# The last product's operand split is moved into the fourth product, the last norm is spread out and done in place, and two tiles are moved by 32 bytes

## The chip, the cores and the metric

One core of one Trainium2 chip runs the kernel. The metric is the device time in microseconds (us) of one execution, given as the median of several runs. The engines are TensorE (PE in the profile, with PEld for its weight loads), VectorE (DVE), ScalarE (ACT), GpSimd (POOL) and SyncE (SP, which here only issues DMAs).

## The reference

A layer on x of 1024 positions by 1024 features: a token mixer (three head groups, one input projection, one output projection), then a feed-forward block. The change touches the second half:

```python
h = rms_norm(x, g_pre_ff[l]) * (1.0 + sc2) + sh2
f = jnp.square(jax.nn.relu(h @ w_ff1[l])) @ w_ff2[l]
x = x + gt2 * rms_norm(f, g_post_ff[l])
```

`w_ff1` is 1024 x 4096, `w_ff2` 4096 x 1024, all in float32. `rms_norm` of `f` needs the sum of squares over all 1024 features of a position before any element can be scaled.

## The kernel before, in words

**Three matmuls for one.** Float32 operands are split into a high and a low part (fp32r): ScalarE casts the high part (`act_hi`), VectorE subtracts it from the raw value to get the low part. `mm3` then issues three matmuls: high by high, high by low, low by high.

**Seven products for eight.** Both feed-forward matmuls cut their operands into 2 x 2 blocks and compute seven products (M1 to M7) on sums of blocks in place of eight. FF1 (16 blocks b of features, 7 x 12 = 84 matmuls of 512 columns each; 14 of the blocks come in the main loop) takes as moving operand either the tile `HL` (the split `h` itself) or `hc` (sums of its blocks), and as weights `wc`. It writes its squared outputs to DRAM as `Y`. FF2 runs the products in the order M1, M5, M6, M4, M7, M3, M2; each adds over 16 values of b, 12 matmuls for each b. A unit `FF2(q, b)` has three steps: `load` (DMAs of a block of Y and of weights into `R`, 1024 columns; where weights are subtracted, a third DMA into `o`), `prep` (subtraction `R<-R,o`, then the split) and `step` (matmuls). The first six products split into pool tiles `x` and use 512 columns.

**The last product, M2**, splits its right operand (block b21 of Y) into `HL`, whose old content is no longer needed, and its weights into tiles `w`, which are kept. It runs in 256-column pieces: piece 0 over all 16 b's, then piece 1 over the same `HL` and `w`, m by m. Its loads and splits stand in the same queues, unit after unit, as all others.

**The last norm** goes in three column pieces, pc 0 (columns 0 to 511, complete when M3 is), pc 1 (512 to 767) and pc 2 (768 to 1023). `square(pc, j)` squares a quarter of the piece into `fq` (ScalarE), adds it to an earlier one, and scales `big` by the gain `g2` in place (ScalarE). `preload(pc)` reads the residual back from `out_dram` into tiles `xh`. `finish` sums over the partitions by matmuls with `ones` (`r<-ones,fq`), takes root and reciprocal, spreads the result by a matmul on a diagonal (`r<-dgt,ones`), multiplies `big` by it into `res`, adds `xh`, and writes `res` out. `FW` is a delay in program order: so much other work is issued before the next part. `behind()` places the norm's matmuls between those of the products.

**Order.** Every engine runs its instructions in the written order. A loop over units calls `load` some units ahead of `step` (`LA`: 5 in FF2) and `prep` 3 ahead. In M2's unit b = 0 the kernel before issues all four `square(0, j)`, `preload(0)` and the start of `finish` for pc 0. Tiles come from a pool: `t` (4 KB, for R, x, w, xh, res), `r` (4 buffers, for o), `h`. `HL` and `big` are fixed tiles ahead of the pool.

Of the kernel before, what the change touches and what calls it, by code (L numbers as in the profile page):

```python
# [21 lines left out]
RS = ((4.1, 2.0, 3.1, 2.1, 4.2), (3.1, 2.0, 2.6, 1.1, 3.7), (2.6, 2.0, 2.6, 0.6, 0.7))  # L22
SEQ = 'f0 f1 z02 a0 a1 b0 b1 z12 z42 z52'
WE = 'GGGGGGGG'
GD = ('GG GG GG GG', 'GV GV', 'V V V V')
NS = (2, 2, 4)
SEs = 'VGV'
FW = (3.5, 4.5, 1.5)
WB = (768,)
LA = (9, 2, 5, 3)  # L30
HY = (2.1, 0.7, 1.4)
REs = ('VG', 'VG', 'VV')
XEs = ('GV', 'VG', 'GV')
# [22 lines left out]
def trunk(ctx, tc, xT, c, pv, ident, w_ada, w_k, w_in, w_v, gates, k1, k2, k3, gmft, w_out, w_ff1, w_ff2, out):  # L56
# [6 lines left out]
    def tt(name, dt=F32, n=1024):  # L63
        return pool.tile([128, n], dt, tag="t", name=name)
# [4 lines left out]
    def pb(name="pb"):  # L69
        return psum.tile([128, 512], F32, tag="b", name=name)  # L70
# [8 lines left out]
    def ctile(name, n, dt=F32, bufs=1):  # L79
        return const.tile([128, n], dt, name=name, tag=name, bufs=bufs)  # L80
# [1019 lines left out]
    class FF2:  # L1100
# [3 lines left out]
        def load(self):  # L1104
            q, b = self.q, self.b
            ra, rb = w_ff2[2 * b], w_ff2[2 * b + 1]
            a11, a12, a21, a22 = ra[:, 0:512], rb[:, 0:512], ra[:, 512:1024], rb[:, 512:1024]
            R = self.R = tt("R")
            self.o = pool.tile([128, 512], F32, tag="r", name="o", bufs=4) if q in ("M5", "M6", "M7", "M3") else None
            nc.sync.dma_start(out=R[:, 0:512], in_=Y[b][:, YB[XS[q]], :])  # L1110
            two = {"M1": (a11,), "M2": (a12,), "M4": (a22,), "M5": (a21, a22), "M6": (SS[b][:, 0, :], a11),
                   "M7": (a11, a21), "M3": (a12, SS[b][:, 1, :])}[q]
            ld[0] = nc.sync.dma_start(out=R[:, 512:1024], in_=two[0]).ins
            if self.o is not None:
                ld[0] = nc.sync.dma_start(out=self.o, in_=two[1]).ins

        def prep(self):
            q, b, R = self.q, self.b, self.R
            w = R[:, 512:1024]
            if self.o is not None:  # L1120
                V.tensor_tensor(out=w, in0=w, in1=self.o, op=ADD if q == "M5" else SUB)  # L1121
                if q in ("M5", "M6"):
                    nc.sync.dma_start(out=SS[b][:, 0 if q == "M5" else 1, :], in_=w)
            if q == "M2":
                x = HL[:, b // 2, b % 2, :]
                act_hi(x[:, 0:512], R[:, 0:512])
                V.tensor_tensor(out=x[:, 512:1024], in0=R[:, 0:512], in1=x[:, 0:512], op=SUB)
                t = hlsplit(w, V, "w2")
                self.X, self.W = (x[:, 0:512], x[:, 512:1024]), t
            else:  # L1130
                hi, lo = wide(R, "x2")
                self.X, self.W = (hi[:, 0:512], lo[:, 0:512]), (hi[:, 512:1024], lo[:, 512:1024])

        def step(self):
            q, b = self.q, self.b
# [38 lines left out]
                mm3([o], wh[:, cs], wl[:, cs], [xs], b == 0 and m % 2 == 0, b == 15, m % 2 == 1)  # L1174


    SE = [{'V': V, 'G': G}[c] for c in SEs]
    sums = {0: [], 1: [], 2: []}

    def square(pc, j):  # L1180

        lo, hi = PIECE[pc]
        g = 512 // (hi - lo)
        a = big[:, j * g:j * g + g, lo:hi]
        q = th("fq")
# [21 lines left out]
    def finish(sums, lo, hi, wait, spec, hold=()):  # L1207
        n = hi - lo
        g, c = 512 // n, n // 128
        spec = spec.split()  # L1210
        xin, at = xins[lo], 8 * lo
        r = pb("r3")
        yield wait
        if lo in WB:
            parts = [t[:, e * n:e * n + n] for t in sums for e in range(g)]
            with behind():
                for j, t in enumerate(parts):
                    mm(r[:, 0:n], ones, t, j == 0, j == len(parts) - 1)
            rr = th("rr", F32, n)
            A.activation(out=rr, in_=r[:, 0:n], func=AF.Sqrt, scale=1.0 / D, bias=eps)  # L1220
            V.reciprocal(rr, rr)
        else:
            with behind():
                for i in range(c):
                    parts = [t[:, e * n + i * 128:e * n + i * 128 + 128] for t in sums for e in range(g)]
                    for j, t in enumerate(parts):
                        mm(r[:, i:i + 1], t, ones[:, 0:1], j == 0, j == len(parts) - 1)
            sd = ctile("sd", 8, bufs=4)
            dg = th("dgt", F32, n)
            A.activation(out=sd[:, 0:c], in_=r[:, 0:c], func=AF.Sqrt, scale=1.0 / D, bias=eps)  # L1230
# [9 lines left out]
        m, rs = 0, None  # L1240
        for i, q in enumerate(spec):
            res = tt("res", F32, 512 * len(q))
            for j, e in enumerate(q):
                o = res[:, j * 512:j * 512 + 512]
                src = rr
                if e in "QR" and lo not in WB:
                    if rs is None:
                        rs = th("rs", F32, n)
                        A.copy(rs, rr)
                    src = rs  # L1250
                (G if e in "QR" else V).tensor_tensor(  # L1251
                    out=o.rearrange("p (m s) -> p m s", m=g), in0=big[:, m:m + g, lo:hi],
                    in1=src.unsqueeze(1).to_broadcast([128, g, n]), op=MUL)
                (G if e in "GQ" else V).tensor_tensor(out=o, in0=o, in1=xin[i][:, j * 512:j * 512 + 512], op=ADD)  # L1254
# [32 lines left out]
    LD1, LP1, LD2, LP2 = LA  # L1287
# [159 lines left out]
```

## Time and profile before

| what | us |
|---|---|
| median of 3 runs (lowest, highest) | 1057.7 (1057.0, 1058.6) |
| the profiled execution | 1055.82 |
| its span | 1054.0 |
| PE busy in it | 981.3 (93%) |
| DVE, ACT, POOL busy in it | 760.6, 507.5, 143.0 |
| 16 DMA engines: mean rate | 182 GB/s |

The span runs from the first to the last instruction that the profiler recorded; 1.8 us of the profiled execution lie around it. Busy times are those of one execution. FF1 and the seven products of FF2 fill the span from 394.81 us to 1039.4 us; the output of the last norm piece ends it.

### The profile page before, as it was taken

How to read it: one execution, taken by the hardware profiler on the slowest of the kernel's cores; microseconds unless marked ns; L12 is line 12 of the kernel's file. 1: busy time of each engine (PE TensorE's matmuls, PEld its weight loads, DVE VectorE, ACT ScalarE, POOL GpSimd, SP SyncE). 2: the span in 40 equal slices, each digit the busy share in tenths (PEclk: the TensorE clock that was granted, in tenths of full speed). 3: DMA queues.
4: the chain of work that ended last, by engine and by line, in shares of the span. 5: the costliest groups of instructions: out<-in, count | busy, mean ns of one | idle time of the engine just before them, and what ended most of it. 6: DMA issues, size and time to landing. Idle time of an engine off the chain costs nothing.

```text
span 1054.0 us, 13168 instructions
## 1 busy us (share of the span) xinstructions
PE 981.3 (93%) x4780; PEld 812.0 (77%) x4780; DVE 760.6 (72%) x1043; ACT 507.5 (48%) x772; POOL 143.0 (14%) x94
## 2 busy tenths in 40 slices
PE   6889976997899999999999999999999999999795
PEld 2668764895678988988888888888888888888685
DVE  7978888778795698896667667676665666577654
ACT  4454777623453455555445445455434444355431
POOL 4400391330320340000000000000000000000231
PEclk8989988998899999999999999999999999999898
DMA  8740210266343432163533433368998877778362
GB/s 344 279 145 11 76 40 0 72 247 233 108 157 123 141 110 86 47 229 131 198 114 143 183 130 144 146 240 295 357 396 305 309 255 260 249 225 312 130 210 91
DMA packets 80003, 191.59 MB, mean 182 GB/s; under 512 B 8769, under 2 KB 13121, under 8 KB 77890
## 3 DMA queue, kind: packets, MB, share of 16 engines
q1 hardware_dynamic: 76482, 186.56, 50.1%
q10 hardware_dynamic: 3456, 4.20, 1.1%
q8 instruction: 37, 0.61, 0.2%
q14 instruction: 28, 0.23, 0.1%
HBM read 144.58 MB, written 46.14 MB: 181 GB/s over the span
## 4 chain that ended last, share of the span: by engine, by line
PE 73%; DVE 13%; DMA 5%; ACT 4%; issue 2%; POOL 1%; SPq 0%; DVEq 0%; POOLq 0%; ACTq 0%
PE f L142 56%; PE op L142 7%; PE zk L142 4%; DVE raw L453 3%; DMA raw<-in_w_ada_dram 3%; PE z L142 2%; PE r L142 2%; DMA R<-in_w_ff_dram 1%; PE grs L142 1%; DVE xr L480 1%; DVE big L536 1%; ACT av L518 1%; DMA xh<-in_xT_dram 1%; DVE ti L538 1%; DMA big<-in_xT_dram 1%
## 5 line engine op out<-in xcount | busy, mean ns | idle before, releaser
L142 PE MATMUL f<-x,x 128*128 128x512 f32 x768 | 236.4, 389 | 0.0
L142 PEld LDWEIGHTS f<-x,x 128*128 128x128 f32 x768 | 144.2, 188 | 29.9
L936 ACT CAST x<-R 128x1024 fp32r<-128x1024 f32 x96 | 100.7, 1054 | 128.3 <-DVE R L1121 62.9
L142 PE MATMUL f<-HL,wc 128*128 128x512 f32 x672 | 161.8, 396 | 0.0
L142 PE MATMUL f<-x 128*128 128x512 f32 x384 | 149.5, 389 | 0.0
L142 PEld LDWEIGHTS f<-HL,wc 128*128 128x128 f32 x672 | 125.1, 188 | 31.5 <-ACT big L1066 2.2
L947 DVE TENSOR_TENSOR x<-R,x 128x1024 fp32r<-128x1024 f32 x96 | 116.6, 1220 | 25.6 <-ACT x L936 22.4
L142 PE MATMUL f<-hc,wc 128*128 128x512 f32 x504 | 119.6, 391 | 0.0
L142 PEld LDWEIGHTS f<-hc,wc 128*128 128x128 f32 x504 | 94.7, 188 | 20.7
L1254 POOL TENSOR_TENSOR res<-res,xh 128x512 f32<-128x512 f32 x10 | 16.3, 1653 | 601.9 <-DVE res L1251 601.9
L142 PE MATMUL op<-HL,hi 128*128 128x256 f32 (+1 forms) x384 | 88.0, 323 | 0.0
L1121 DVE TENSOR_TENSOR R<-R,o 128x512 f32<-128x512 f32 x64 | 44.3, 692 | 59.9 <-DMA R<-in_w_ff_dram 36.9
L142 PEld LDWEIGHTS f<-x 128*128 128x128 f32 x384 | 72.1, 188 | 14.9
L142 PEld LDWEIGHTS op<-HL,hi 128*128 128x128 f32 x384 | 63.5, 188 | 7.3 <-issue 1.4
L170 POOL TENSOR_TENSOR lo<-raw,hi 128x1024 fp32r<-128x1024 f32 x16 | 44.1, 2766 | 158.1 <-ACT hi L169 111.8
L142 PE MATMUL z<-HL,hi 128*128 128x512 f32 x192 | 64.9, 441 | 0.7 <-ACT ftg L613 0.7
L142 PE MATMUL op<-HL,lo 128*128 128x256 f32 (+1 forms) x192 | 61.4, 320 | 0.0
L453 DVE SCALAR_TENSOR_TENSOR raw<-raw,cond 128x1024 f32<-128x1024 f32 x32 | 49.9, 1567 | 13.4 <-DMA raw<-in_w_ada_dram 13.4
L936 ACT CAST wc<-S 128x1024 fp32r<-128x1024 f32 x28 | 29.4, 1052 | 60.7 <-DVE S L1041 57.2
L142 PE MATMUL f<-HL,w 128*128 128x256 f32 x384 | 49.5, 288 | 2.5 <-DVE w L941 2.3
L142 PEld LDWEIGHTS f<-HL,w 128*128 128x128 f32 x384 | 47.5, 194 | 3.9 <-DVE w L941 2.9
L947 DVE TENSOR_TENSOR wc<-S,wc 128x1024 fp32r<-128x1024 f32 x28 | 34.2, 1221 | 21.8 <-PE f L142 20.0
(299 smaller groups left out, 1695.3 us busy)
## 6 DMA issues: line engine op xcount, KB each, us to landing
R<-Y SPq DMA_DIRECT2D x112, 256.0 KB, 4.6
raw<-in_w_ada_dram SPq DMA_DIRECT2D x48, 512.0 KB, 4.7
R<-in_w_ff_dram SPq DMA_DIRECT2D x96, 256.0 KB, 4.5
raw<-in_w_ff_dram SPq DMA_DIRECT2D x32, 512.0 KB, 3.2
Y<-big SPq DMA_DIRECT2D x16, 1024.0 KB, 3.9
o<-in_w_ff_dram SPq DMA_DIRECT2D x48, 256.0 KB, 5.0
Y<-big SPq DMA_DIRECT2D x13, 768.0 KB, 3.5
SS<-R SPq DMA_DIRECT2D x32, 256.0 KB, 5.0
```

What stands on the lines that cost most here:

```text
L142: pe[0] = T.matmul(o, w, x, start=start, stop=stop, skip_group_check=more).ins
L170: (eng or V).tensor_tensor(out=lo, in0=src, in1=hi, op=SUB)
L453: V.scalar_tensor_tensor(out=r, in0=r, scalar=0.5, in1=cond, op0=MUL, op1=MUL, accum_out=mod[:, blk:blk + 1])
L480: V.scalar_tensor_tensor(out=xr[:, o0:o1], in0=z[:, i0:i1], scalar=col("conv_w", k * 4 + t), in1=xr[:, o0:o1], op0=MUL, op1=ADD)
L518: A.activation(out=av[:, a:b], in_=rr[h], func=AF.Exp, scale=m4[:, i:i + 1], bias=m4[:, i:i + 1])
L536: V.tensor_tensor_scan(ti, av, ti, 0.0, op0=MUL, op1=ADD)
L538: V.tensor_tensor_scan(ti[:, ::-1], av[:, ::-1], ti[:, ::-1], 0.0, op0=MUL, op1=ADD)
L936: order[0] = A.copy(dst, src).ins
L947: V.tensor_tensor(out=lo, in0=raw, in1=hi, op=SUB)
L1121: V.tensor_tensor(out=w, in0=w, in1=self.o, op=ADD if q == "M5" else SUB)
L1254: (G if e in "GQ" else V).tensor_tensor(out=o, in0=o, in1=xin[i][:, j * 512:j * 512 + 512], op=ADD)
```

## The change

It does five things.
- M4 (the fourth product) loads block b21 of Y beside its own operands, into `o`, and splits it into `HL` there (16 casts, 16 subtractions). M2 then loads only weights (256 KB per unit, into `o`, for 512 KB into `R`) and splits only these. `LA` gets two more numbers: loads 7 units ahead and preps 4 ahead for M2's 16 units.
- The squares of pc 0 are spread over M2's units b = 1 to 4; `preload(0)` and `finish` for pc 0 start at b = 7. All additions of squares are on VectorE, into one tile for a piece (two for pc 2), so that there are fewer norm matmuls.
- The gain g2 of pc 0 is no longer multiplied on ScalarE but inside `finish`, in one VectorE instruction with the norm's factor.
- `finish` works in place: `big` times the factor into `big`, plus `xh` into `xh`, which is written out. `res` is gone, and so is all work of GpSimd at the end.
- 32 bytes are put ahead of `HL` and 32 behind `big`. As built, `HL` moves from address 3456 to 3488, `big` from 68992 to 69024, and the pool's first tile from 102240 to 102304 (in each partition).

```diff
@@ constants and tiles @@
-GD = ('GG GG GG GG', 'GV GV', 'V V V V')
-NS = (2, 2, 4)
-SEs = 'VGV'
+GD = ('VV VV VV VV', 'VV VV', 'V V V V')
-LA = (9, 2, 5, 3)
+LA = (9, 2, 5, 3, 7, 4)
+    ctile("pad0", 8)
     HL = const.tile([128, 8, 2, 1024], F32R, name="HL", tag="HL")
     big = const.tile([128, 8, 1024], F32, name="big", tag="big")
+    ctile("pad1", 8)
@@ FF2.load @@
...
+            self.o = pool.tile([128, 512], F32, tag="r", name="o", bufs=4) if q != "M1" else None
+            if q == "M2":
+                ld[0] = nc.sync.dma_start(out=self.o, in_=a12).ins
+                return
...
-            two = {"M1": (a11,), "M2": (a12,), "M4": (a22,), "M5": (a21, a22), "M6": (SS[b][:, 0, :], a11),
+            two = {"M1": (a11,), "M4": (a22, Y[b][:, YB["b21"], :]), "M5": (a21, a22),
...
@@ FF2.prep @@
+            x = HL[:, b // 2, b % 2, :]
+            if q == "M2":
+                self.X, self.W = (x[:, 0:512], x[:, 512:1024]), hlsplit(self.o, V, "w2")
+                return
...
-            if q == "M2":
-                x = HL[:, b // 2, b % 2, :]
-                act_hi(x[:, 0:512], R[:, 0:512])
-                V.tensor_tensor(out=x[:, 512:1024], in0=R[:, 0:512], in1=x[:, 0:512], op=SUB)
-                t = hlsplit(w, V, "w2")
-                self.X, self.W = (x[:, 0:512], x[:, 512:1024]), t
...
+            if q == "M4":
+                act_hi(x[:, 0:512], self.o)
+                V.tensor_tensor(out=x[:, 512:1024], in0=self.o, in1=x[:, 0:512], op=SUB)
@@ square @@
-        if len(sums[pc]) < NS[pc]:
+        if not sums[pc] or (pc == 2 and j == 1):
             sums[pc].append(q)
         else:
-            i = j % NS[pc]
-            SE[pc].tensor_tensor(out=sums[pc][i], in0=sums[pc][i], in1=q, op=ADD)
-        for m in range(j * g, j * g + g):
+            V.tensor_tensor(out=sums[pc][0], in0=sums[pc][0], in1=q, op=ADD)
+        for m in range(j * g, j * g + g if pc else 0):
             A.activation(out=big[:, m, lo:hi], in_=big[:, m, lo:hi], func=AF.Copy, scale=g2[:, m:m + 1])
@@ finish @@
...
-            res = tt("res", F32, 512 * len(q))
...
+                o, x = big[:, m:m + g, lo:hi], xin[i][:, j * 512:j * 512 + 512]
+                if g == 1:
+                    V.scalar_tensor_tensor(out=o[:, 0], in0=o[:, 0], scalar=g2[:, m:m + 1], in1=rr, op0=MUL, op1=MUL)
+                else:
+                    V.tensor_tensor(out=o, in0=o, in1=rr.unsqueeze(1).to_broadcast([128, g, n]), op=MUL)
+                (G if e == "G" else V).tensor_tensor(out=x.rearrange("p (m s) -> p m s", m=g), in0=o,
+                                                     in1=x.rearrange("p (m s) -> p m s", m=g), op=ADD)
...
-            nc.sync.dma_start(out=out[:, at:at + 512 * len(q)], in_=res)
+            nc.sync.dma_start(out=out[:, at:at + 512 * len(q)], in_=xin[i])
@@ the loop over units @@
...
+    def ahead(u, a, b, c):
+        return a if u < n1 else b if u < len(units) - 16 else c
...
-        while lo_ <= u + LD2 and (lo_ <= u + LD1 or lo_ >= n1):
+        while lo_ <= u + ahead(lo_, LD1, LD2, LD3):
...
-            for j in range(4):
-                square(0, j)
-            preload(0)
-            tf = [spawn(finish(sums[0], 0, 512, FW[0], GD[0]), 0.0)]
+        if o.q == "M2":
+            if 1 <= o.b < 5:
+                square(0, o.b - 1)
+            if o.b == 7:
+                preload(0)
+                tf = [spawn(finish(sums[0], 0, 512, FW[0], GD[0]), 0.0)]
```

On TensorE, in M2's piece 0, the sums of pc 0's squares stood behind the third unit (each unit has twelve matmuls, two rows; `w_...` names its weights):

```order
L142 MATMUL f_7666<-HL,w_7638 128x256 x6
L142 MATMUL r_7696<-ones,fq 128x1 x8
L142 MATMUL f_7665<-HL,w_7662 128x256 x6
L142 MATMUL f_7666<-HL,w_7662 128x256 x6
L142 MATMUL f_7665<-HL,w_7711 128x256 x3
L142 MATMUL r_7696<-dgt,ones 128x512
```

Now, at the same place of the program, they stand behind the tenth unit (`w_7648` is the first unit's, `w_7821` the tenth's):

```order
L143 MATMUL f_7724<-HL,w_7821 128x256 x6
L143 MATMUL r_7869<-ones,fq 128x1 x4
L143 MATMUL f_7723<-HL,w_7838 128x256 x6
L143 MATMUL f_7724<-HL,w_7838 128x256 x6
L143 MATMUL f_7723<-HL,w_7855 128x256 x3
L143 MATMUL r_7869<-dgt,ones 128x512
```

The norm's matmuls are seven units later, and four in place of eight.

On VectorE, at the end of M3 (`big<-big,f` adds M3's sums to `big`), half of M2's splits stood ahead of M3's sums, and each needed a block of Y and one of weights; behind the norm the other half followed, between the products of `finish`:

```order
L941 TENSOR_TENSOR w_7784<-R,w_7784 128x512
L1127 TENSOR_TENSOR HL<-R,HL 128x512
L1164 TENSOR_TENSOR big<-big,f_7290 128x512
L1164 TENSOR_TENSOR big<-big,f_7291 128x512
L1164 TENSOR_TENSOR big<-big,f_7292 128x512
L1191 TENSOR_TENSOR fq<-fq 128x512
L1164 TENSOR_TENSOR big<-big,f_7293 128x512
L1191 TENSOR_TENSOR fq<-fq 128x512 x3
L1231 RECIPROCAL sd<-sd 128x4
L1232 TENSOR_TENSOR dgt<-idt,sd 128x512
L1251 TENSOR_TENSOR res<-big,r_7696 128x512 x2
L941 TENSOR_TENSOR w_7810<-R,w_7810 128x512
```

Now the first fourteen splits of weights stand ahead of M3's sums, and the last two between the additions of squares:

```order
L942 TENSOR_TENSOR w_7896<-o,w_7896 128x512
L1170 TENSOR_TENSOR big<-big,f_7355 128x512
L1170 TENSOR_TENSOR big<-big,f_7356 128x512
L1170 TENSOR_TENSOR big<-big,f_7357 128x512
L1170 TENSOR_TENSOR big<-big,f_7358 128x512
L1195 TENSOR_TENSOR fq<-fq 128x512
L942 TENSOR_TENSOR w_7920<-o,w_7920 128x512
L1195 TENSOR_TENSOR fq<-fq 128x512
L942 TENSOR_TENSOR w_7935<-o,w_7935 128x512
L1195 TENSOR_TENSOR fq<-fq 128x512 x2
L1235 RECIPROCAL sd<-sd 128x4
```

No split of M2 is left behind the norm, and none needs Y.

On SP's queue, the four reads of the residual (`xh<-out_dram`, 512 KB each) stood behind the sixth of M2's sixteen pairs of loads:

```order
L1110 DMA R<-Y_3018 128x512
L1113 DMA R<-in_w_ff_dram 128x512
L1203 DMA xh<-out_dram 128x1024 x4
L1110 DMA R<-Y_3019 128x512
L1113 DMA R<-in_w_ff_dram 128x512
```

Now they stand behind the fifteenth of M2's sixteen single loads:

```order
L1120 DMA o<-SS_3046 128x512
L1112 DMA o<-in_w_ff_dram 128x512 x15
L1207 DMA xh<-out_dram 128x1024 x4
L1112 DMA o<-in_w_ff_dram 128x512
```

One load is left behind them, where ten pairs were.

## Rows read from the trace of the kernel before

**Rows 1.** Busy time by stretch of the span. Columns: stretch; its length, then the busy time (and instructions) of PE, PEld, DVE, ACT and POOL; the granted TensorE clock; the share of the DMA engines; GB/s. The stretches are: early products, output projection, FF1, the first six products of FF2, M2.

```profile
100.00:290.00 190.00, 161.92 (x813) 133.57 (x813) 155.21 (x183) 109.77 (x164) 67.66 (x39) 0.90 0.31 109
290.00:412.00 122.00, 117.79 (x708) 102.04 (x708) 93.03 (x167) 57.77 (x124) 31.62 (x27) 1.00 0.40 132
412.00:712.00 300.00, 300.00 (x1394) 246.61 (x1393) 218.81 (x309) 149.84 (x221) 0.00 (x0) 1.00 0.40 151
712.00:974.00 262.00, 262.00 (x1158) 217.07 (x1157) 168.78 (x186) 120.81 (x142) 0.00 (x0) 1.00 0.86 296
974.00:1039.40 65.40, 55.21 (x421) 53.06 (x420) 35.65 (x49) 21.97 (x39) 18.85 (x12) 0.92 0.44 155
```

**Rows 2.** The chain of work that ended last. Columns: start, duration, engine, what.

```profile
412.03 559.26 PE f L142 x2535
971.34 7.13 DMA R<-in_w_ff_dram
...
1039.57 3.47 PE r L142 x16
```

**Rows 3.** Timeline of PE in M2 and the tail. Columns: start, duration, engine, line, operation, output and operands, shape, count; in brackets the idle time before and what ended it. Each float32 norm matmul has two records.

```profile
973.85 4.36 PE L142 MATMUL f<-HL,w 128*128 128x256 f32 x36
985.10 0.59 PE L142 MATMUL r<-ones,fq 128*128 128x1 f32 x2 [6.89 <-DVE fq L1191]
986.38 3.15 PE L142 MATMUL r<-ones,fq 128*128 128x1 f32 x14 [0.69 <-DVE fq L1191]
...
992.73 1.09 PE L142 MATMUL r<-dgt,ones 128*128 128x512 f32 x2
993.26 8.93 PE L142 MATMUL f<-HL,w 128*128 128x256 f32 x71
...
1021.10 1.50 PE L142 MATMUL r<-ones,fq 128*128 128x1 f32 x12
1022.46 1.30 PE L142 MATMUL f<-HL,w 128*128 128x256 f32 x9
1023.70 0.67 PE L142 MATMUL r<-dgt,ones 128*128 128x256 f32 x2
1024.02 15.55 PE L142 MATMUL f<-HL,w 128*128 128x256 f32 x129
1039.40 3.62 PE L142 MATMUL r<-fq,ones 128*128 128x256 f32 x16
```

**Rows 4.** Timeline of SP's queue around the residual reads.

```profile
965.30 4.57 SPq L1203 DMA_DIRECT2D xh<-out_dram  x4
```

**Rows 5.** Timeline of ACT at M2's start.

```profile
976.45 0.62 ACT L936 CAST HL<-R 128x512 fp32r<-128x512 f32 x1 [5.42 <-DMA R<-Y]
```

**Rows 6.** Timeline of DVE at M2's start.

```profile
977.11 0.69 DVE L1127 TENSOR_TENSOR HL<-R,HL 128x512 fp32r<-128x512 f32 x1 [5.35 <-ACT HL L936]
...
980.43 1.88 DVE L1164 TENSOR_TENSOR big<-big,f 128x512 f32<-128x512 f32 x3
```

**Rows 7.** DMA issues of the page: line engine op xcount, KB each, median us from issue to landing.

```profile
o<-in_w_ff_dram SPq DMA_DIRECT2D x48, 256.0 KB, 5.0
...
xh<-out_dram SPq DMA_DIRECT2D x6, 512.0 KB, 6.6
```

**Rows 8.** Timeline of PE where FF1 ends and FF2 begins (columns as in Rows 3): the moving operand changes from `HL` to `x`.

```profile
707.09 5.77 PE L142 MATMUL f<-HL,wc 128*128 128x512 f32 x24
712.69 0.40 PE L142 MATMUL f<-x 128*128 128x512 f32 x1
...
714.09 0.39 PE L142 MATMUL f<-x 128*128 128x512 f32 x1
...
730.41 0.39 PE L142 MATMUL f<-x 128*128 128x512 f32 x1
```

**Rows 9.** Timeline of SP's queue in FF1: the raw weights of two blocks after each other, each load held back until the block before frees its buffers.

```profile
513.08 6.34 SPq L163 DMA_DIRECT2D raw<-in_w_ff_dram  x2
...
532.52 6.34 SPq L163 DMA_DIRECT2D raw<-in_w_ff_dram  x2
```

**Rows 10.** The costliest groups of PE, shapes kept apart: line engine op, names, shapes, count | busy us, mean ns | idle before.

```profile
L142 PE MATMUL f<-HL,wc 128*128 128x512 f32 x672 | 161.8, 396 | 0.0
L142 PE MATMUL z<-HL,hi 128*128 128x512 f32 x192 | 64.9, 441 | 0.7 <-ACT ftg L613 0.7
...
L142 PE MATMUL op<-HL,hi 128*128 128x512 f32 x128 | 41.0, 400 | 0.0
```

**Rows 11.** Timeline of all engines in the tail (columns as in Rows 3).

```profile
1040.39 0.63 ACT L1186 ACTIVATE fq<-big 128x512 f32<-128x512 f32 x1 [9.80 <-DVE big L1343]
...
1043.12 0.47 ACT L1220 ACTIVATE rr<-r,eps 128x256 f32<-128x256 f32 x1 [1.16 <-PE r L142]
```

**Rows 12.** Busy time by stretch as in Rows 1: M4 alone.

```profile
843.00:887.00 44.00, 44.00 (x195) 36.46 (x195) 27.68 (x28) 18.70 (x19) 0.00 (x0) 1.00 0.78 254
```

**Rows 13.** Timeline of DVE in M3: the split of its unit b = 8, and the last two splits.

```profile
946.02 1.23 DVE L947 TENSOR_TENSOR x<-R,x 128x1024 fp32r<-128x1024 f32 x1 [0.94 <-ACT x L936]
...
958.98 2.54 DVE L947 TENSOR_TENSOR x<-R,x 128x1024 fp32r<-128x1024 f32 x2 [0.20 <-ACT x L936]
```

**Rows 14.** Timeline of PE in M3: the first matmuls of its units b = 8 and b = 15.

```profile
952.09 0.39 PE L142 MATMUL f<-x 128*128 128x512 f32 x1
...
971.13 0.39 PE L142 MATMUL f<-x 128*128 128x512 f32 x1
```

More of the change, by code (lines that the diff above doesn't have):

```diff
@@ L1107, in load @@
             a11, a12, a21, a22 = ra[:, 0:512], rb[:, 0:512], ra[:, 512:1024], rb[:, 512:1024]
+            self.o = pool.tile([128, 512], F32, tag="r", name="o", bufs=4) if q != "M1" else None
+            if q == "M2":
+                ld[0] = nc.sync.dma_start(out=self.o, in_=a12).ins
+                return
             R = self.R = tt("R")
-            self.o = pool.tile([128, 512], F32, tag="r", name="o", bufs=4) if q in ("M5", "M6", "M7", "M3") else None
             nc.sync.dma_start(out=R[:, 0:512], in_=Y[b][:, YB[XS[q]], :])
-            two = {"M1": (a11,), "M2": (a12,), "M4": (a22,), "M5": (a21, a22), "M6": (SS[b][:, 0, :], a11),
-                   "M7": (a11, a21), "M3": (a12, SS[b][:, 1, :])}[q]
+            two = {"M1": (a11,), "M4": (a22, Y[b][:, YB["b21"], :]), "M5": (a21, a22),
+                   "M6": (SS[b][:, 0, :], a11), "M7": (a11, a21), "M3": (a12, SS[b][:, 1, :])}[q]
             ld[0] = nc.sync.dma_start(out=R[:, 512:1024], in_=two[0]).ins
@@ L1117, in prep @@
         def prep(self):
-            q, b, R = self.q, self.b, self.R
+            q, b = self.q, self.b
+            x = HL[:, b // 2, b % 2, :]
+            if q == "M2":
+                self.X, self.W = (x[:, 0:512], x[:, 512:1024]), hlsplit(self.o, V, "w2")
+                return
+            R = self.R
             w = R[:, 512:1024]
-            if self.o is not None:
+            if q not in ("M1", "M4"):
                 V.tensor_tensor(out=w, in0=w, in1=self.o, op=ADD if q == "M5" else SUB)
@@ L1123, in prep @@
                     nc.sync.dma_start(out=SS[b][:, 0 if q == "M5" else 1, :], in_=w)
-            if q == "M2":
-                x = HL[:, b // 2, b % 2, :]
-                act_hi(x[:, 0:512], R[:, 0:512])
-                V.tensor_tensor(out=x[:, 512:1024], in0=R[:, 0:512], in1=x[:, 0:512], op=SUB)
-                t = hlsplit(w, V, "w2")
-                self.X, self.W = (x[:, 0:512], x[:, 512:1024]), t
-            else:
-                hi, lo = wide(R, "x2")
-                self.X, self.W = (hi[:, 0:512], lo[:, 0:512]), (hi[:, 512:1024], lo[:, 512:1024])
+            hi, lo = wide(R, "x2")
+            self.X, self.W = (hi[:, 0:512], lo[:, 0:512]), (hi[:, 512:1024], lo[:, 512:1024])
+            if q == "M4":
+                act_hi(x[:, 0:512], self.o)
+                V.tensor_tensor(out=x[:, 512:1024], in0=self.o, in1=x[:, 0:512], op=SUB)
         def step(self):
@@ L1174, in piece @@
                 mm3([o], wh[:, cs], wl[:, cs], [xs], b == 0 and m % 2 == 0, b == 15, m % 2 == 1)
-    SE = [{'V': V, 'G': G}[c] for c in SEs]
     sums = {0: [], 1: [], 2: []}
@@ L1239, in finish @@
         yield from hold
-        m, rs = 0, None
+        m = 0
         for i, q in enumerate(spec):
-            res = tt("res", F32, 512 * len(q))
             for j, e in enumerate(q):
[L1244 to L1254, printed above, removed]
+                o, x = big[:, m:m + g, lo:hi], xin[i][:, j * 512:j * 512 + 512]
[5 more added lines that the diff above has]
+                                                     in1=x.rearrange("p (m s) -> p m s", m=g), op=ADD)
                 m += g
                 yield 0.9
-            nc.sync.dma_start(out=out[:, at:at + 512 * len(q)], in_=res)
+            nc.sync.dma_start(out=out[:, at:at + 512 * len(q)], in_=xin[i])
             at += 512 * len(q)
@@ L1285, in trunk @@
         pend.append(y_out(b, c11, c12, c21, c22, slab(2 + b), [(c12, 0, 1), (c22, 1, 1), (c21, 2, 1)]))
-    LD1, LP1, LD2, LP2 = LA
+    LD1, LP1, LD2, LP2, LD3, LP3 = LA
     units = [(o, i) for o in b1s for i in range(7)][2:] + [(o, None) for o in b2s]
@@ L1302, in do_prep @@
             o.prep() if i is None else o.prep(i)
+    def ahead(u, a, b, c):
+        return a if u < n1 else b if u < len(units) - 16 else c
     lo_, pr_ = 1, 1
     for u, (o, i) in enumerate(units):
-        while lo_ <= u + LD2 and (lo_ <= u + LD1 or lo_ >= n1):
+        while lo_ <= u + ahead(lo_, LD1, LD2, LD3):
             do_load(lo_)
             lo_ += 1
-        while pr_ <= u + LP2 and (pr_ <= u + LP1 or pr_ >= n1):
+        while pr_ <= u + ahead(pr_, LP1, LP2, LP3):
             do_prep(pr_)
```

## The prediction

> **What bounds the kernel now.** I read the busy time by stretch first [rows 1]. From 412 to 974 us PE is busy all the time at a granted clock of 1.00: FF1 and the first six products of FF2 are bound by the issue of matmuls, and only shorter matmuls can shorten them. M2 is different: of 65.40 us PE is busy 55.21, its clock is 0.92, and DVE, ACT and POOL are all far from full. The chain of waits says the same: 559.26 us of matmuls without a break, then a DMA of weights of 7.13 us for M2, and at the end the norm's 16 matmul records [rows 2].
>
> The timeline of PE says where M2 loses [rows 3]. It begins at 973.85 and ends at 1039.40, 65.55 us. Its own products run at (1039.40 - 1024.02) / 129 = 119.2 ns where nothing disturbs them, so 384 of them need 45.8 us. PE stops for 6.89 us ahead of `r<-ones,fq`, which stands behind three units, and waits there for squares. Going back from there: on SP's queue 2 MB of residual reads stand in the middle of M2's loads [rows 4]; ACT idles 5.42 us for a block of Y, and casts it only at 976.45 [rows 5]; DVE, in order, does that unit's splits and the two behind it, and so adds M3's sums to `big` only from 980.43 [rows 6], though M3 ended at about 974. Squares, additions and the norm's matmuls follow. So the stop is a queueing effect and not a lack of data for the products. Behind it PE runs slowly for a while (the norm's 14 records take 3.00 us, 214 ns each; twelve such records take 1.36, 113 each, at 1021.10).
>
> **M2 after.** The products need 45.8 us as before. The norm matmuls inside M2: two groups of 8 records at 113 ns, 1.8 us, and two spreads, 993.26 - 992.73 = 0.53 and 1024.02 - 1023.70 = 0.32, together 2.7 us [rows 3].
>
> Does PE still wait at the first norm? It now comes behind ten units, at 973.85 + 10 x 12 x 0.1192 = 988.2. On DVE fourteen splits of weights stand ahead of M3's sums. There are four `o` buffers; one round of four takes 5.0 us from issue to landing [rows 7] plus a cast of 0.62 and a subtraction of 0.69 (the same shapes as in [rows 5, 6]), 6.3 us. The first four are loaded while M3's last units are split. M3's last split ended at 958.98 + 2.54 = 961.5, 9.6 us before PE needed it [rows 13, 14]. From there four splits take 2.8 us and three more rounds 18.9 at most: the fourteenth is done at about 982, M3's four sums (1.88 us for three) at 984.5. The last two squares stand on ACT behind the cast of the sixteenth load, which waits in the queue for the residual reads: issued at about 977, landed 6.6 us later [rows 7], so about 985, then a load, a cast, two squares and two additions, some 3 us: 988. That is level with PE. I take 0; if M3's splits had only the lead of their worst unit, 952.09 - (946.02 + 1.23) = 4.8 us [rows 13, 14], all of it would come 4 us later, and that is the bound. The products need the last split by 973.85 + 15 x 1.43 = 995, which either case meets.
>
> The second norm: the spread of pc 0 ends at about 991.7, then DVE does 16 in-place instructions at 0.63 us (the sums' time [rows 6]), 10.1 us, before piece 0's sums, squares and additions, some 3.3 us: 1005.1. PE arrives there after 192 products, the first norm and 62 more products: 973.85 + 22.9 + 1.4 + 7.4 = 1005.5. That is level, and I add 0.5 us. The cover is piece 1's products; without it, a DVE late by x makes PE late by x. M2 thus takes 45.8 + 2.7 + 0.5 = 49.0 and **16.5 us** are saved (13 if the first norm waits, 17 with no wait).
>
> **The tail.** Sixteen records of 3.47 / 16 = 217 ns become eight [rows 2]. Four can run before the last square, which ends at 1040.39 + 0.63 = 1041.02; the other four then take 0.9, and the root, now at 1043.12 [rows 11], starts at about 1042.0: **1.1 us**. What follows keeps its eight operations.
>
> **M4's extra work.** M4 gets 16 x 0.62 = 9.9 us on ACT and 16 x 0.69 = 11.0 on DVE. In its 44 us these are busy 18.70 and 27.68 [rows 12], so both fit (28.6 and 38.7). DMA goes from 512 to 768 KB per unit, which the other products carry. PE is covered by the lead of the splits; I cost it at **0**. If the fuller queues cost 0.3 us of lead per unit, 16 units would take 4.8 us, just what M3 has left at its lowest, unit 8 [rows 13, 14]: the bound is a stall of 5 us. In the program as built, `R` of M7 reuses buffers freed five units before and no longer three, which speaks for more lead, not less. FF1's earlier loads change nothing: each already waits for a buffer [rows 9].
>
> **The 32 bytes.** The matmuls with `HL` as moving operand take (712.69 - 707.09) / 24 = 233.3 ns, those with `x`, straight behind them at the same clock, (730.41 - 714.09) / 72 = 226.7 [rows 8]. Both load their weights from the pool; the moving tile differs. Before, `HL` lies 32 bytes off the pool's grid (3456 and 102240, modulo 512), `x` and its weights on one grid; after, `HL` is on it too (3488 and 102304). So I take it that `HL` then gets the time of `x`. An FF1 block has a period of 532.52 - 513.08 = 19.44 us [rows 9]; 84 matmuls at 226.7 would be 19.04: 14 blocks, 5.6 us. The other 512-column matmuls with `HL` at full clock on a busy PE are those of the output projection and the first two FF1 blocks between 290 and 412 us [rows 1, 10], about 260 at 7 ns: 1.8. Those of the early products (`z` and the like, about 400 [rows 10]) lie where the clock is 0.90 and PE idles [rows 1]: 0, bound 2.7. The 256-column ones need 119.2 ns against 113 for the one-column matmuls, so at most 6 ns each can go; for M2's 384 and as many earlier I take 2 ns, 1.5 us, bounds 0 and 5. Sum **8.9 us**, bounds 0 and 15.
>
> [...]
>
> **Sum.** 16.5 + 1.1 + 8.9 = 26.5 us from the profiled execution's 1055.8 (span 1054.0 and 1.8 around it): 1029.3. The median of the runs is 1.9 above that execution, so the median forecast is 1031.
>
> **The rivals.** *The 32 bytes do nothing* (0.20). The 6.6 ns could belong to where `HL` lies or to how its rows are cut, and not to the grid; nothing in this trace varies the address alone. Then 1031 + 8.9 = 1040.
>
> *Part of M2's gain comes back* (0.12). M3's splits lose their lead to M4's loads (5 us), or the fourteen splits ahead of M3's sums come late (4 us): 1035 to 1040. For it speaks the 4.8 us of lead; against it that ten units now lie between.
>
> *Slower* (0.04). The pool moves too, by 64 bytes, so all other matmuls get new addresses. If the 1656 matmuls on `x` and `hc` went up by twice what separates `HL` from `x`, 13.2 ns, and `HL` gained nothing, that is +21.9 on 1040: 1062. It decides from 17.6 / 1656 = 10.6 ns on. Against it: two streams on the pool's grid keep their distance to each other, and they are the fast ones.
>
> *No change* (0.02): M2's stop only moves to the second norm, the clock falls there instead, and the 32 bytes are worth nothing.
>
> **How the numbers follow.** The forecast itself has 0.62, with its own range 1026 to 1035. The range for 8 in 10 goes down to 1024 (the bounds of the 32 bytes) and up to 1042, which takes in the rivals at 1035 to 1040. A measurement of this kernel tells about 0.2% (2 us) from no change: faster 0.62 + 0.20 + 0.12 = 0.94, same 0.02, slower 0.04.
>
> **What the profile after would show.** M2 from its first product to the last norm in about 49 us, no stop of PE over 1 us, clock near 1.00 in it; if a stop ahead of `r<-ones,fq` stays, M3's sums on DVE are late. `HL` streams at 227 ns and an FF1 block in 19.0 us; if 233 and 19.44 stay, the first rival holds. The splits of M3 at least 4 us ahead of PE; if not, M4's extra loads are the cause. POOL idle after 412 us. The prediction is wrong above all if the 32 bytes do something other than bring `HL` to the time of `x`.

## The result and the profile after

The changed kernel takes 1030.3 us (median of 6 runs, 1028.9 to 1033.0) against 1057.35 for the kernel before in the same sittings; the ratio is 0.9752, 95% interval 0.9729 to 0.9775. The forecast was 1031, with a range of 1024 to 1042. The profiled execution took 1031.33, its span is 1029.5. One execution of the kernel a_pool below took 1608.63 us at a mean granted clock of 0.561 and is left out of its figures.

The span by stage, worked out from the start of the first matmul of each stage (the end of M2 is the start of the last norm's first matmul):

| stage | before | after | saved | forecast |
|---|---|---|---|---|
| to FF1's main loop | 440.57 | 438.29 | 2.3 | 1.8 |
| FF1's 14 blocks | 272.12 | 267.61 | 4.5 | 5.6 |
| FF2, six products | 261.16 | 261.12 | 0.0 | 0 |
| M2 | 65.55 | 49.40 | 16.15 | 16.5, and a part of 1.5 for shorter 256-column matmuls in all stages |
| tail | 14.6 | 13.1 | 1.5 | 1.1 |

The longest piece of the changed kernel's chain of waits (start, duration, engine, what) answers to [rows 2], where M2 began with a DMA of 7.13 us. It reaches into M2, and no DMA stands in the chain behind it:

```profile
409.26 572.32 PE f L143 x2667
```

Busy time by stretch (columns as in [rows 1]): M2 in three thirds. PE is busy throughout, and its granted clock is 1.00 where it was 0.92.

```profile
968.00:984.00 16.00, 16.00 (x137) 16.00 (x136) 4.90 (x9) 1.94 (x4) 0.00 (x0) 1.00 0.14 47
984.00:1000.00 16.00, 16.00 (x132) 15.52 (x130) 12.75 (x20) 2.97 (x6) 0.00 (x0) 1.00 0.55 198
1000.00:1016.00 16.00, 15.95 (x131) 15.72 (x131) 6.77 (x12) 1.80 (x4) 0.00 (x0) 1.00 0.29 100
```

The timeline of PE in M2 and the tail, which answers to [rows 3]. There is no bracket (no idle time) before the norm's matmuls; the eight records of each norm's sums take 0.81 us (982.23 - 981.42).

```profile
967.02 14.55 PE L143 MATMUL f<-HL,w 128*128 128x256 f32 x120
981.42 0.95 PE L143 MATMUL r<-ones,fq 128*128 128x1 f32 x8
982.23 2.04 PE L143 MATMUL f<-HL,w 128*128 128x256 f32 x15
984.10 1.02 PE L143 MATMUL r<-dgt,ones 128*128 128x512 f32 x2
984.56 14.84 PE L143 MATMUL f<-HL,w 128*128 128x256 f32 x119
999.23 0.95 PE L143 MATMUL r<-ones,fq 128*128 128x1 f32 x8
...
1001.61 14.97 PE L143 MATMUL f<-HL,w 128*128 128x256 f32 x122
1016.42 1.02 PE L143 MATMUL r<-fq,ones 128*128 128x256 f32 x4
1018.02 1.13 PE L143 MATMUL r<-fq,ones 128*128 128x256 f32 x4 [0.58 <-ACT fq L1191]
```

On DVE (same columns) M3's sums come at 965.77, while M3 still runs, and the last addition of squares ends at 971.84 + 1.48 = 973.3: 8 us before PE asks for it at 981.42. Before, M3's sums came only at 980.43, 6.6 us after M3's end [rows 6].

```profile
965.16 0.69 DVE L942 TENSOR_TENSOR w<-o,w 128x512 fp32r<-128x512 f32 x1 [2.03 <-ACT w L937]
965.77 2.47 DVE L1170 TENSOR_TENSOR big<-big,f 128x512 f32<-128x512 f32 x4
...
971.84 1.48 DVE L1195 TENSOR_TENSOR fq<-fq 128x512 f32<-128x512 f32 x2
```

The change of the moving operand from `HL` to `x`, which answers to [rows 8]: (705.90 - 700.47) / 24 = 226.3 ns for `HL`, where it was 233.3.

```profile
700.47 5.60 PE L143 MATMUL f<-HL,wc 128*128 128x512 f32 x24
705.90 0.39 PE L143 MATMUL f<-x 128*128 128x512 f32 x1
```

SP's queue in FF1, which answers to [rows 9]: a block takes 528.78 - 509.67 = 19.11 us, where it took 19.44.

```profile
509.67 6.25 SPq L164 DMA_DIRECT2D raw<-in_w_ff_dram  x2
...
528.78 6.25 SPq L164 DMA_DIRECT2D raw<-in_w_ff_dram  x2
```

### The profile page after: what moved, and what is told of

It reads as the page before. It is cut to its first block, busy times and chain, and to the rows that moved or that the text cites. A ratio compares the mean times of both kernels' runs of the same rounds, so it can differ in the third digit from the quotient of the medians.

```text
span 1029.5 us, 13104 instructions
## 1 busy us (share of the span) xinstructions
PE 963.3 (94%) x4756; PEld 804.0 (78%) x4756; DVE 766.4 (74%) x1059; ACT 501.0 (49%) x764; POOL 123.8 (12%) x82
## 3 DMA queue, kind: packets, MB, share of 16 engines
q10 hardware_dynamic: 3456, 4.20, 1.1%
## 4 chain that ended last, share of the span: by engine, by line
PE 73%; DVE 14%; DMA 4%; ACT 4%; issue 3%; POOL 1%; SPq 0%; DVEq 0%; POOLq 0%
PE f L143 59%; PE op L143 6%; DMA raw<-in_w_ada_dram 3%; DVE raw L454 2%; PE z L143 2%; PE zk L143 2%; PE grs L143 1%; PE r L143 1%; DVE raw L291 1%; DVE HL L325 1%; DVE xr L481 1%; DVE big L537 1%; DMA big<-in_xT_dram 1%; ACT av L519 1%; DVE ss L279 1%
## 5 line engine op out<-in xcount | busy, mean ns | idle before, releaser
L143 PE MATMUL f<-HL,wc 128*128 128x512 f32 x672 | 158.1, 390 | 0.0
L143 PEld LDWEIGHTS z<-HL,hi 128*128 128x128 f32 x192 | 38.5, 204 | 11.9 <-issue 3.7
```

The source lines that it names most:

```text
L143: pe[0] = T.matmul(o, w, x, start=start, stop=stop, skip_group_check=more).ins
```

## The experiments

### The 32 bytes: distance or place

Four kernels made from the kernel before, with paddings alone (`ctile` counts in floats of 4 bytes, so 8 are 32 bytes):

```diff
+    ctile("pad0", 8)    # p_both, p_ahead
     HL = const.tile([128, 8, 2, 1024], F32R, name="HL", tag="HL")
     big = const.tile([128, 8, 1024], F32, name="big", tag="big")
+    ctile("pad1", 8)    # p_both, p_behind; 24 in p_64
```

> The kernel before with the two paddings of 32 bytes and nothing else. Theory (the distance between HL and the pool, 0 modulo 512 bytes, sets the matmul's time): HL streams of 512 columns at 227 ns where they were at 234, an FF1 block in 19.1 to 19.2 us, FF1 4 us shorter and the output projection and early products 2 to 3 us shorter together; time 1050 to 1052. Rival (the paddings are worth nothing and the shorter streams of the changed kernel come from its other edits): 234 ns stays, 1057.

> The kernel before with the padding behind big alone: HL stays at 3456, the pool moves from 102240 to 102272, so their distance is 0 modulo 512. Theory (the distance counts): 227 ns for HL streams. Rival (HL's own address counts, whether it is a multiple of 64): 234 ns stays.

> The kernel before with the padding ahead of HL alone: HL moves to 3488 and the pool to 102272, so their distance is what it was, 32 short of a multiple of 512. Theory (the distance counts): 234 ns stays, 1057. Rival (HL's own address counts): 227 ns.

> The kernel before with 96 bytes behind big: HL at 3456, the pool at 102336, distance 64 modulo 512. If only the distance modulo 64 counts: 227 ns, as with distance 0. [...]

With both paddings: 1052.75 us, ratio 0.994 (0.9915 to 0.9964). The other three ran once each: p_behind 1052.31, p_ahead 1057.53, p_64 1062.09 us. The groups of PE with shapes kept apart (busy us, mean ns) for p_both, p_behind, p_ahead and p_64 in turn; [rows 10] has 396 for the kernel before:

```profile
L144 PE MATMUL f<-HL,wc 128*128 128x512 f32 x672 | 157.9, 390 | 0.0
```

```profile
L143 PE MATMUL f<-HL,wc 128*128 128x512 f32 x672 | 158.0, 390 | 0.0
```

```profile
L143 PE MATMUL f<-HL,wc 128*128 128x512 f32 x672 | 161.8, 396 | 0.0
```

```profile
L143 PE MATMUL f<-HL,wc 128*128 128x512 f32 x672 | 161.7, 395 | 0.0
```

A mean of 390 goes with a spacing (start to start, median) of 227 ns, 396 with 234, 395 with 233. p_behind leaves `HL` where it was and gains; p_ahead moves `HL` as the change does and does not. So what counts is the distance between the moving operand and the weights: 0 modulo 512 bytes is good, 32 short and 64 over are not. FF1 took 272.12 us before and 267.45 with both paddings: 4.7 us; with p_behind 267.48, with p_ahead 272.21.

A fifth kernel, made from the changed one, tries a distance of 256:

```diff
-    sp = ctile("sp", 64)
...
     ctile("pad1", 8)
+    sp = ctile("sp", 64)
```

> The changed kernel with the tile sp (256 bytes) behind big in place of ahead of HL: HL at 3232, the pool at 102304, distance 256 modulo 512. If the distance counts modulo 256 or less: 227 ns for HL streams of 512 columns, 120 for 256, time 1030. [...]

```profile
L143 PE MATMUL f<-HL,wc 128*128 128x512 f32 x672 | 158.0, 390 | 0.0
```

The time was 1030.26 us (one run), and the spacing is 227 ns again: distance 256 is as good as 0, and by p_64 distance 64 is not. Whether the time repeats in steps of 256 bytes or of 128 was not tried.

### The paddings and the 256-column matmuls

> The changed kernel without the two paddings. Theory (the distance of HL and the pool is worth what it was in the kernel before): HL streams of 512 columns at 234 ns, time 1036 to 1038, M2 unchanged or 0.5 us shorter, since its 256-column matmuls were 118 ns off the grid and 120 on it. Rival (M2's gain needs the paddings): M2 longer than 51 us.

```diff
-    ctile("pad0", 8)
-    ctile("pad1", 8)
```

1036.45 us, ratio 0.9783 (0.9761 to 0.9806). PE's timeline in M2 of this kernel:

```profile
974.16 14.16 PE L141 MATMUL f<-HL,w 128*128 128x256 f32 x120
...
1008.09 14.59 PE L141 MATMUL f<-HL,w 128*128 128x256 f32 x122
1022.52 1.02 PE L141 MATMUL r<-fq,ones 128*128 128x256 f32 x4
```

The last 122 products take (1022.52 - 1008.09) / 122 = 118.3 ns each; in the changed kernel it is (1016.42 - 1001.61) / 122 = 121.4. M2 is 48.36 us here and 49.40 there. The paddings help the 512-column matmuls on `HL` in FF1 (mean 390 ns there, 395 here) and harm the 256-column ones. A further kernel takes both advantages: it keeps FF1 at distance 0 and writes M2's operand 32 bytes further on.

```diff
-    HL = const.tile([128, 8, 2, 1024], F32R, name="HL", tag="HL")
+    HLf = const.tile([128, 16392], F32R, name="HL", tag="HL")
+    HL = HLf[:, 0:16384].rearrange("p (a b c) -> p a b c", a=8, b=2)
...
-            x = HL[:, b // 2, b % 2, :]
+            x = HLf[:, 8 + b * 1024:8 + b * 1024 + 1024]
```

(The padding behind `big` is taken out, so that the pool stays where it is.)

> The changed kernel with HL eight floats longer and M2's right operand written 32 bytes further on in it, so that the 512-column matmuls of FF1 keep the distance 0 and the 256-column ones of M2 get a distance of 32 bytes. Theory (distance 0 is the best one for 512 columns and the worst for 256): HL streams of FF1 stay at 227 ns, M2's matmuls go from 120 to 118 ns, M2 from 49.4 to 48.4 us, time 1 us below the changed kernel, which is less than the runs can tell. Rival (the 118 ns came from the place of the weights in the pool, not from the distance): M2 stays at 49.4.

```profile
965.12 14.16 PE L143 MATMUL f<-HL,w 128*128 128x256 f32 x120
...
999.04 14.59 PE L143 MATMUL f<-HL,w 128*128 128x256 f32 x122
1013.47 1.02 PE L143 MATMUL r<-fq,ones 128*128 128x256 f32 x4
```

M2 takes 1013.47 - 965.12 = 48.35 us, with 118.3 ns for a product, and FF1 stays at 267.6. The rival falls: the weights have not moved. The time was 1028.92 us, ratio 0.972 (0.9683 to 0.9757), which cannot be told from the changed kernel's; the microsecond is seen in the trace alone.

### What frees M2

Three kernels made from the changed one undo the place of the norm, the place of the split, and both. a_norm0:

```diff
-            if 1 <= o.b < 5:
-                square(0, o.b - 1)
-            if o.b == 7:
-                preload(0)
-                tf = [spawn(finish(sums[0], 0, 512, FW[0], GD[0]), 0.0)]
+        if o.q == "M2" and o.b == 0:
+            for j in range(4):
+                square(0, j)
+            preload(0)
+            tf = [spawn(finish(sums[0], 0, 512, FW[0], GD[0]), 0.0)]
```

a_split2 (a_both has this and the edit above):

```diff
-            if q == "M2":
-                ld[0] = nc.sync.dma_start(out=self.o, in_=a12).ins
-                return
-            two = {"M1": (a11,), "M4": (a22, Y[b][:, YB["b21"], :]), "M5": (a21, a22),
+            two = {"M1": (a11,), "M2": (a12,), "M4": (a22,), "M5": (a21, a22),
...
+            if q == "M2":
+                act_hi(x[:, 0:512], R[:, 0:512])
+                V.tensor_tensor(out=x[:, 512:1024], in0=R[:, 0:512], in1=x[:, 0:512], op=SUB)
+                self.X, self.W = (x[:, 0:512], x[:, 512:1024]), hlsplit(w, V, "w2")
+                return
```

> The changed kernel with pc 0's four squares, the residual reads and the start of its norm back at M2's unit b = 0; the right operand stays split in M4. The first norm then stands behind four units in place of ten, at M2's start + 5.8 us; in the changed kernel its data were ready at M2's start + 6.3. Theory (the moved split is what frees VectorE; the norm's later place is only reserve): PE waits 0 to 2 us, time 1030 to 1033. Rival (the later place is what hides the norm): PE waits 5 us or more and its clock falls, 1037 to 1041.

> The changed kernel with the right operand loaded and split in M2 as before (two loads and four splitting operations for a unit), the norm still behind ten units and the residual reads still late. Theory (the split is what delays M3's sums): the sums come 5 to 8 us later than in the changed kernel, the first norm's data at M2's start + 12 to 16, PE waits 0 to 3 us there or for splits, 1031 to 1035. Rival (the place of the norm and of the residual reads alone is enough): no wait, 1030.

> Both of these undone together: split in M2, norm and residual reads at b = 0. Theory (each of the two alone covers the stop, so that their gains do not add): PE stops 6 to 9 us ahead of the first norm, its clock falls, M2 takes 60 to 65 us, 1041 to 1046. Rival (one of them carries the gain alone): the same time as the worse of the two single ones.

| kernel | median us | ratio to the kernel before (95%) | M2 in the profile |
|---|---|---|---|
| after | 1030.3 | 0.9752 (0.9729 to 0.9775) | 49.40 |
| a_norm0 | 1034.62 | 0.9771 (0.9749 to 0.9792) | 53.55 |
| a_split2 | 1036.83 | 0.9792 (0.975 to 0.9835) | 54.43 |
| a_both | 1042.94 | 0.9853 (0.9818 to 0.9888) | 57.74 |
| p_both | 1052.75 | 0.994 (0.9915 to 0.9964) | 67.70 |

The M2 of this table is that of one profiled execution each. The time of a_norm0 lies between its theory (1030 to 1033) and its rival (1037 to 1041), that of a_split2 above both of its own (1031 to 1035, 1030); a_both's is in the range of its theory (1041 to 1046), but its M2 is shorter than 60 to 65 us.

In a_norm0 PE waits 2.60 us for the squares, and then its granted clock is 0.72 for 6 us (PE's timeline; the clock is the number before the DMA share in the second fence):

```profile
975.27 1.05 PE L143 MATMUL r<-ones,fq 128*128 128x1 f32 x8 [2.60 <-DVE fq L1195]
976.19 2.60 PE L143 MATMUL f<-HL,w 128*128 128x256 f32 x11
```

```profile
976.00:982.00 6.00, 6.00 (x33) 5.24 (x34) 2.66 (x5) 0.26 (x1) 0.00 (x0) 0.72 0.01 3
```

The last addition ends 7.9 us after M2's start (975.22 - 967.36) and PE asks 5.3 us after it. In the changed kernel the data are there after 6.3 us, so about 1.0 us of the 2.60 comes from the norm's place alone. The other 1.6 us go with late weights: the residual reads are back in the middle of M2's loads, and a load issued right behind them at 953.46 is cast only at 962.85, 9.4 us later, where such loads took 5.0 from issue to landing in the kernel before [rows 7]. ACT's timeline:

```profile
962.85 2.59 ACT L937 CAST w<-o 128x512 fp32r<-128x512 f32 x4 [5.55 <-DMA o<-in_w_ff_dram]
```

In a_split2 the first norm's sums are in time, but the next step, `dgt`, is not, and PE waits for that. On ACT the last unit's casts stand ahead of the root in the program, and they need a block of Y. That block is loaded behind the residual reads: issued at 975.08, cast at 984.30, 9.2 us later. On DVE that unit's two subtractions stand ahead of `dgt` (PE's timeline, then ACT's and DVE's):

```profile
987.30 2.04 PE L143 MATMUL r<-dgt,ones 128*128 128x512 f32 x2 [3.40 <-DVE dgt L1231]
```

```profile
984.30 0.62 ACT L937 CAST HL<-R 128x512 fp32r<-128x512 f32 x1 [1.48 <-DMA R<-Y]
```

```profile
984.95 0.69 DVE L1125 TENSOR_TENSOR HL<-R,HL 128x512 fp32r<-128x512 f32 x1 [1.40 <-ACT HL L937]
...
986.46 0.69 DVE L1231 TENSOR_TENSOR dgt<-idt,sd 128x512 f32<-128x512 f32 x1
```

With both undone PE stops 5.76 us and its granted clock is 0.54 in the stretch behind (PE's timeline, then the stretch):

```profile
977.78 1.87 PE L143 MATMUL r<-ones,fq 128*128 128x1 f32 x8 [5.76 <-DVE fq L1190]
```

```profile
978.00:984.00 6.00, 6.00 (x27) 5.60 (x27) 2.89 (x6) 1.29 (x3) 0.00 (x0) 0.54 0.36 113
```

In a_both M3's sums on DVE are in time, 0.3 us after M2's start (966.71). What is late are the squares: on ACT they stand behind a cast that waits for a block of Y, again one that was loaded behind the residual reads (issued at 963.95; DVE's timeline, then ACT's):

```profile
967.03 2.48 DVE L1165 TENSOR_TENSOR big<-big,f 128x512 f32<-128x512 f32 x4
```

```profile
971.50 0.62 ACT L937 CAST HL<-R 128x512 fp32r<-128x512 f32 x1 [5.11 <-DMA R<-Y]
```

My expectation of a cover that either edit gives alone fell: in M2 one undone costs 4.2 us, the other 5.0, both 8.3. Whether the gains add is less sure. The profiled execution of a_both was the fastest of its four (1039.37 for a median of 1042.94), and by the ratios to the kernel before (their differences times 1058) the costs are 2, 4 and 11 us, each known to a few us only. Nor are the causes two separate queues: in all three kernels the wait goes back to loads that stand behind the residual reads on SP's queue, and with the split in M2 blocks of Y are among them.

### GpSimd's additions, and what is left

a_both with two more edits undone (b_pool_la), and the changed kernel with GpSimd's additions alone (a_pool):

```diff
-GD = ('VV VV VV VV', 'VV VV', 'V V V V')    # both kernels
+GD = ('GG GG GG GG', 'GV GV', 'V V V V')
-LA = (9, 2, 5, 3, 7, 4)                     # b_pool_la
+LA = (9, 2, 5, 3, 5, 3)
```

> The changed kernel with the residual's additions of pc 0 (all eight) and pc 1 (half) back on GpSimd, still in place. Theory (these additions hurt only where VectorE has splits with two SBUF operands beside them, and here the splits are over by then): M2 stays within 1 us of 49.4, time 1030 to 1031. Rival (GpSimd's additions slow VectorE's in-place products too, and so delay the second norm): second norm's matmuls wait 2 us or more, 1032 to 1035.

> The kernel with both of M2's moves undone (split in M2, norm at b = 0), which ran at a ratio of 0.985 to the kernel before, with two more edits undone: the additions of pc 0 and half of pc 1 on GpSimd again, and loads and preps of M2 5 and 3 units ahead again. What is left of the change against the kernel before is the paddings, the sums on VectorE into one tile, the gain in the norm's instruction and the missing res tiles. Theory (GpSimd's additions stretch the splits beside them, and shorter look-ahead starves them): M2 64 to 68 us, 1049 to 1053. Rival (the res tiles and ScalarE's scaling were what cost): M2 58 to 61 us, 1040 to 1044.

a_pool: 1030.19 us, ratio 0.9731 (0.9677 to 0.9784), which cannot be told from the changed kernel's; M2 1015.94 - 966.83 = 49.11 us. PE's timeline:

```profile
966.83 8.44 PE L143 MATMUL f<-HL,w 128*128 128x256 f32 x69
...
1015.94 1.02 PE L143 MATMUL r<-fq,ones 128*128 128x256 f32 x4
```

Taking GpSimd out of the end is worth nothing that these runs can tell once no split stands beside it. b_pool_la: 1045.29 us, ratio 0.9873 (0.9833 to 0.9914), M2 63.38 us. It lies between my two expectations, and its interval overlaps that of a_both. GpSimd's additions do stretch the splits beside them, to as much as 1.79 us here and 1.78 in the kernel before (DVE's timeline; the same subtraction takes 0.69 alone, and the products of `big` and `r` between them take 0.67 to 0.69 in the kernel before), but PE waits only 0.46 us for one of them; the larger part is the first stop (PE's timeline, then DVE's):

```profile
993.54 1.79 DVE L1125 TENSOR_TENSOR HL<-R,HL 128x512 fp32r<-128x512 f32 x1
995.25 1.79 DVE L942 TENSOR_TENSOR w<-R,w 128x512 fp32r<-128x512 f32 x1
```

```profile
980.73 1.87 PE L143 MATMUL r<-ones,fq 128*128 128x1 f32 x8 [10.74 <-DVE fq L1190]
```

```profile
970.06 0.69 DVE L1125 TENSOR_TENSOR HL<-R,HL 128x512 fp32r<-128x512 f32 x1 [5.00 <-ACT HL L937]
```

GpSimd has no part in that stop: it ends at 980.73, and GpSimd's first addition in M2 starts at 988.00. On DVE splits that wait for late blocks of Y stand ahead of M3's sums here, which come 9.2 us after M2's start (973.39 - 964.20); in a_both they came after 0.3. That points to the look-ahead, which was not changed alone. The stop also differs from kernel to kernel with the same M2: in one execution each of the kernel before and of p_both, p_behind, p_ahead and p_64 it was 6.89, 8.51, 11.18, 9.43 and 10.69 us, and M2 65.6 to 71.5. So of the 5.6 us between b_pool_la and a_both (63.38 and 57.74) 5.0 are the first stop (10.74 and 5.76), by the look-ahead or by this spread, and 0.46 the wait beside GpSimd's additions.

Between p_both and b_pool_la (1052.75 and 1045.29) lie the sums of squares on VectorE into fewer tiles, with fewer norm matmuls, the gain in the norm's instruction and the missing `res` tiles. Of it the traces show the tail (1.5 us) and the norm matmuls of M2, which after the stop take 1.7 us for 8 records and 0.8 for the next 8, where p_both's 16 and 16 took 4.3 and 1.8. That is 3.6 of the 4.3 us between their M2s (67.70 and 63.38). The edits were not tried one by one.

## Why the prediction was right, and where its steps were off

**The place and the sum.** M2's loss was read right: it was PE's idle time and what went with it. M2 fell to 49.40 us; forecast were 49.0, or about 48.2 with its half of the 1.5 us for shorter 256-column matmuls. Of the 16.15 us saved, 10.2 were idle time of PE (65.40 - 55.21 in [rows 1], nothing over 0.1 us now), 3.8 the sums of the norm (5.4 us for 32 records, 1.6 for 16), and 2.1 the products, which took 49.1 us with a part at the lower clock and take 46.9. FF1 moved by the length of its matmuls and the six products of FF2 not at all. Total forecast 26.5 us, measured between the two profiled spans 24.5, between the medians 27.

**The first norm** was put level with PE (988 us on the old scale, bound 4 us late). It came 8 us early. The step that failed is the place of M3's last split: I kept it where it was, 12.3 us ahead of M2's start (961.5 and 973.85), and let the fourteen splits take up to 21.7 us from there. It ended 19.5 us ahead (947.52 and 967.02), and the fourteen took 18.3, so that they are over at 965.85, before M3 ends:

```profile
946.30 1.22 DVE L948 TENSOR_TENSOR x<-R,x 128x1024 fp32r<-128x1024 f32 x1 [1.16 <-ACT x L937]
947.44 2.49 DVE L942 TENSOR_TENSOR w<-o,w 128x512 fp32r<-128x512 f32 x4
```

The moved split itself gives M3 this lead: in the changed kernel M3's splits end 12.7 us or more before PE's first matmul of the unit (in a_norm0 12.4, in a_pool 12.2, in a_nopad 11.5), where the least was 4.8 in the kernel before; with the split back in M2 it is 2.3 in a_split2, 4.8 in a_both and 3.3 in b_pool_la. The prediction only remarked that M7's buffers speak for more lead, and gave it no time.

**The second norm** was put level too, with 0.5 us: there is no idle time before its sums at 999.23, but its last addition ends only at 998.84, so this term was read rightly and there is 0.4 us to spare. **M4's extra work** was put at nothing, and the six products take 261.12 us for 261.16. It did cost lead: M4's splits end at least 6.1 us ahead of PE, where it was 11.6.

**The tail.** 1.1 us forecast; the root starts 2.77 us after M2's end (1019.19), where it took 3.72: 0.95. The other 0.5 us lie behind the root.

```profile
1019.19 0.47 ACT L1224 ACTIVATE rr<-r,eps 128x256 f32<-128x256 f32 x1 [0.28 <-PE r L143]
```

**The 32 bytes.** The mechanism (the distance to the pool) was right and its rival is out: p_behind and p_ahead decide it. The sizes were off. FF1 gave 4.5 us for 5.6: I let every matmul of a block have the time of `x`, but in the changed kernel the first five of a run on `HL` behind four on `hc` are slower (272, 236, 228, 233, 230 ns start to start, in most blocks). The 256-column matmuls were forecast to gain 2 ns each and lost 2 to 3: of the term of +1.5 us half lay in M2, and there it was about -1.0. So the products of M2 take 46.9 us where 45.8 were reckoned. It had no row, only the remark that 119.2 stands above 113, and the range's lower bound of nothing left out a loss. The front gained 2.3 us in this pair; over all kernels here, one execution each, it is 437.5 us on average with distance 0 or 256 (ten kernels, 435.6 to 438.5) and 440.7 without (four, 439.9 to 441.3).

**The clock.** That PE idles and then is granted less (0.51 from 985 to 993 us in the kernel before, behind the stop of 6.89) showed up again in a_norm0 (0.72 behind 2.60), a_split2 (0.72 from 988 to 992 us, behind the stop of 3.40) and a_both (0.54 behind 5.76); the slow matmuls behind the stop were, as the sum assumed, a part of what M2 lost.

**Luck.** The terms come to 24.5 us in the profiled pair, 2 less than forecast; that the medians differ by 27 is in part luck. The profiled execution of before lies 1.5 us under its median (1055.82 and 1057.35), that of after 1.0 over its own (1031.33 and 1030.3), and the forecast was reckoned from the former. Which stages make these differences is not shown. One candidate for the first is M2: the profiled 65.55 us is the shortest of the five old M2s (65.6 to 71.5). Inside M2 the products were 1.1 us longer than reckoned, and the norm's matmuls (2.4 us for 2.7) and the wait at the second norm (0 for 0.5) shorter, which nearly cancels.

## What to carry to other kernels

Where a queue serves several purposes in order, ask of each wait what stands ahead of it on that queue: here two megabytes of reads in the middle of the last product's loads, and the splits that waited for those loads ahead of a norm, cost PE some 8 us, the lower clock behind the stop included. Moving the reads with the norm, or the split, takes away only a part; it took both to leave no stop. Work that needs only early data (a split of an operand that is ready) belongs where its engine has holes. And where two streams of matmuls with the same shape differ in time, compare the addresses of their operands: moving the pool by 32 bytes was worth 4.6 us in FF1 (p_behind), and the two paddings cost the 256-column matmuls of M2 about 1 (49.40 us of M2, 48.36 in a_nopad).

## What the runs showed of the hardware

- In this kernel's streams, with new weights for each matmul, matmuls of 512 columns on `HL` in FF1 are spaced (median) by 227 ns when the moving operand and the weights lie 0 or 256 bytes apart modulo 512 (the changed kernel, a_256), 234 when 32 short (the kernel before) and 233 when 64 over (p_64). With 256 columns 0 is the slower one: in M2 the median is 120 ns at 0 (the changed kernel) and 118 when 32 short (the kernel before), and the last 122 products took 121.4 ns each at 0 and 256 (the changed kernel, a_256) and 118.3 when 32 short (a_nopad, a_m2off). Why the two sizes differ stays open.
- A stop of PE of 2.60 us was followed by 6 us at a mean granted clock of 0.72 (a_norm0), one of 5.76 by 6 us at 0.54 (a_both); the stretch behind each was at 1.00 again (8 us and 6 us).
- A load of 256 KB issued right behind four reads of 512 KB on SP's queue was cast 7.5, 9.2 and 9.4 us after its issue (a_both, a_split2, a_norm0); the weights' median from issue to landing was 5.0 in the kernel before.
- The stage that waits on queues took 65.6 to 71.5 us in one execution each of five kernels with the same code for it; without waits it took 49.40, 49.11 and 49.39 in three (the changed kernel, a_pool and a_256).
